# A hybrid decoder layer: one level of Strassen's algorithm for the queries and values of the last 512 tokens

## The chip, the cores and the metric

The kernel runs on one core of a Trainium2 chip. TensorE (PE) multiplies, VectorE (DVE), ScalarE (ACT) and GpSimd (POOL) do elementwise work, and SyncE (SP) issues nearly all transfers as one queue in program order. The metric is the device time of one execution in microseconds (us). A measurement of this kernel can tell about 0.2% (1.65 us) from no change.

## The reference

Each of 2048 tokens has 1024 channels, all in float32. What the change touches is the combined input projection:

```python
h = (rmsnorm(x, g_norm[l]).astype(jnp.float32) * (1.0 + scale[:, None, :]) + shift[:, None, :]).astype(x.dtype)
proj = jnp.einsum('bsd,de->bse', h, w_in[l])
gq, gk, gv, ga, gz, sq, sk, sv, sz = split_cols(proj, COL_SIZES)
...
q = rope(sq.reshape(B, S, SWA_Q_HEADS, SWA_HEAD_DIM), positions)
k = rope(sk.reshape(B, S, SWA_KV_HEADS, SWA_HEAD_DIM), positions)
o_swa = sliding_window_sink_attention(q, k, v, sinks[l])
o_swa = (o_swa.astype(jnp.float32) * jax.nn.silu(sz.astype(jnp.float32))).astype(x.dtype)
y = jnp.einsum('bse,ed->bsd', jnp.concatenate([o_gla, o_swa], axis=-1), w_out[l])
x = (x.astype(jnp.float32) + gate[:, None, :] * y.astype(jnp.float32)).astype(x.dtype)
```

`gv` holds the values (512 columns) of the gated linear attention (GLA), whose queries and keys are `gq`, `gk`, decay input `ga` and gate `gz`. `sq` holds the 512 query columns of the sliding window attention (SWA), which rope rotates; `sk`, `sv` are its keys and values and `sz` its gate.

## The kernel before

**Units and slots.** The tokens are worked through in four units of 512 (unit 0 to 3). A unit multiplies its normalized input by the columns of `w_in` in nine slots, in the order of the list `ORDER`. A slot is one group of columns: `sz0`, `sz1`, `gz0`, `gz1`, `qk0`, `qk1` (256 each, function `proj_t`, PSUM tile `pt`), `kv` (272), `sq` and `gv` (512 each, function `proj_n`, PSUM tile `pn`). After the units an output stage (`out_pair`, tiles `ya` and `ys`) multiplies by `w_out`, already by seven Strassen products in place of eight for all but the first pair of token tiles.

**Products.** Every float32 operand is split in a high and a low part of type float32r: `hh`, `hl` for the input (8 tiles of 128 channels by 512 tokens), and two parts for the weights. One product is three matmuls:

```python
def mm3(ps, lh, ll, rh, rl, first, last, bank=None):
    mmul(ps, lh, rh, first, False, bank)
    mmul(ps, lh, rl, False, False)
    mmul(ps, ll, rh, False, last)
```

So `sq` and `gv` take 4 token tiles x 8 channel tiles x 3 = 96 matmuls each in a unit, of 512 columns each. They alternate between two PSUM banks (`mm`).

**Weights.** Unit 0 splits the weights and writes the parts to DRAM (`wc`). Later units load them as tiles of 1 MB, each in two transfers, into a ring of five buffers (`w_tile`, `WB = 5`): a load waits until the last matmul that reads the tile five loads earlier.

**What follows a slot.** The queries are rotated by DVE and POOL (`rope`), the values are copied by ACT. As soon as the slots that they need are done, SWA is computed per token tile (`swa_tile`, PSUM tiles `pq`, `psc`, `ppt`, `ppo`) and GLA per pair of heads (`gla`, tiles `pk`, `pc`, `pu`, `po`, `pms`). Results go to DRAM (`mixd`). `norm` makes the next unit's `hh` and `hl`. They live in a pool of 13 buffers of each kind (`hp`, `HB = 13`): 8 for a unit, 5 for the start of the next.

**Late work.** The output stage's weights are combined at low priority inside units 1 and 2: `late_gate`, then `late_rows(k)` for k = 0 to 3, which load four blocks of `w_out` (`wor`), multiply them on DVE, form combinations on POOL, split them on ACT and DVE and store them (`woc`). The table `LATE_AT` says after which slot each piece may begin. `last_rows` loads them back (`woh`, `wol`).

**Order.** All calls are recorded (class `Order`), and a list scheduler with durations of its own fixes each engine's instruction order before the program is built. `od.lift` shifts the priority of what is recorded next. Helpers record everything, so the profile shows one line for all calls (L390) and two for PE (L441, L446); tiles tell them apart.

Of the kernel before, what the change touches and what calls it, by code (L numbers as in the profile page):

```python
# [395 lines left out]
def layer_kernel(ctx, tc, small, x, xT, w_ada, w_gate, b_gate, w_in, w_dec, w_out, g_fin, out):  # L396
# [14 lines left out]
    const = Pool("const", 1)  # L411
    hp = Pool("hp", HB)
    wp = Pool("wp", 1)
# [202 lines left out]
    def last_rows():  # L616
# [7 lines left out]
        for op in WO:  # L624
            for k in range(KT // 2):
                wo[op, k] = []
                for j in range(2):
                    name = f"wo{'hl'[j]}{op}{k}"
                    if op == WO[3] and k == KT // 2 - 3:
                        t = keep.tile([P, NB], F32R, name=name, tag="wst", bufs=4)  # L630
                    elif op == WO[3] and k >= KT // 2 - 2:
                        t = spare[:, k - KT // 2 + 2, j]
                    elif op in WO[:4]:
                        t = hp.tile([P, NB], F32R, name=name, tag=f"h{'hl'[j]}")
# [15 lines left out]
    woc = dram.tile([P, 2, len(WO), KT // 2, NB], F32R, name="woc")  # L650
    wo = {}

    def first_w():
# [197 lines left out]

    def norm(u):

# [662 lines left out]
    for i, (u, slot) in enumerate(todo):  # L1516
        if u > 0 and slot == ORDER[0]:
            hh, hl = nexth[u]
        w = ws[i]
        name, _, half = slot.partition("/")  # L1520
        if name == "kv":
            proj_n(w, SLOT_N[name], sink_kv(u))
        elif name == "sq":
            qrs[u] = {}
# [6 lines left out]
        seen.add((u, slot))  # L1531
        if half:
            if not {(u, f"{name}/{c}") for c in range(2)} <= seen:
# [6 lines left out]
        for what, g, need in (("S", 0, ("kv", "sz0", "sq")), ("S", 1, ("kv", "sz1", "sq")),  # L1540
                              ("G", 0, ("qk0", "gv", "kv")), ("G", 1, ("qk1", "gv")),
                              ("Z", 0, ("qk0", "gz0", "gv")), ("Z", 1, ("qk1", "gz1", "gv"))):
            if name in need and all((u, n) in seen for n in need):
                if what == "S":
# [10 lines left out]
        if u < NU - 1 and name == (NORM_AT if u else NORM_AT0):  # L1555
            od.lift = -LIFT
            norm(u + 1)
            od.lift = 0
        if (u, name) in LATE_AT:
            at = LATE_AT[u, name]  # L1560
            od.lift = LATE_LIFT
            late_gate() if at == "gate" else late_rows(at)
            od.lift = 0
# [58 lines left out]
```

## Time and profile before

| | |
|---|---|
| three runs | 826.36, 827.63, 827.90 us; median 827.63 us |
| the profiled execution | 827.18 us, of which the span of its instructions is 825.4 us |
| busy share of the span | PE 98%, weight loads 82%, DVE 71%, ACT 63%, POOL 43% |
| bytes moved | 200.82 MB, mean 243 GB/s |
| granted PE clock | 1.00 after the first 50 us (2.4 GHz) |

The span is what the trace covers; 1.8 us of the execution lie outside it. Unit 1 begins with slot `sz0` at 158.7 us, unit 2 at 330 us, unit 3 at 495.4 us, the output stage at 657 us. Unit 3 runs its slots at 495.4 (`sz0`), 507.0 (`kv`), 525.0 (`sz1`), 537.5 (`sq`), 559.2 (`qk0`), 574.5 (`gv`), 610.8 (`gz0`), 631.3 (`qk1`) and 643.4 (`gz1`).

### The profile page before, as it was taken

To read this page: it belongs to the slowest core of one execution; us is meant where nothing else is said; L and a number is where in the kernel's file an instruction comes from. 1 tells how busy PE (TensorE), PEld (TensorE's weight loads), DVE (VectorE), ACT (ScalarE), POOL (GpSimd) and SP (SyncE) were. 2 spreads that over 40 slices of the span, in tenths; PEclk is the share of its full clock that TensorE was granted. 3 is DMA by queue.
4 is the path that set the end of the run, shared out by engine and by line. 5 is a ranking of instruction groups with operands and counts; after the bars stand their busy time and mean duration, and the time that the engine had idled before them with its cause. 6 is when DMAs were issued, how large, how long until landed. Compare 5 with 4: busy or idle time off the path is not lost.

```text
span 825.4 us, 13307 instructions
## 1 busy us (share of the span) xinstructions
PE 809.1 (98%) x4286; PEld 674.9 (82%) x4286; DVE 587.0 (71%) x1172; ACT 519.2 (63%) x1293; POOL 353.0 (43%) x442
## 2 busy tenths in 40 slices
PE   8899999999999999999999999999999999999996
PEld 7788888898888877888887788888887888888885
DVE  6987567777578878665788836525764857898985
ACT  4769856999457786956587757615866544444432
POOL 3812325566435756446476524332562412233300
PEclk9999999999999999999999999999999999999999
DMA  9979998738285696896978937727376863454432
GB/s 356 371 262 369 383 384 300 252 125 332 90 318 204 228 374 222 264 385 230 328 240 302 325 114 267 259 82 288 122 241 246 292 244 128 154 165 150 152 107 77
DMA packets 92125, 200.82 MB, mean 243 GB/s; under 512 B 9443, under 2 KB 27414, under 8 KB 89366
## 3 DMA queue, kind: packets, MB, share of 16 engines
q1 hardware_dynamic: 91766, 199.69, 68.2%
q8 instruction: 34, 0.56, 0.3%
q14 instruction: 37, 0.30, 0.1%
q10 hardware_dynamic: 288, 0.26, 0.1%
HBM read 145.26 MB, written 54.66 MB: 242 GB/s over the span
## 4 chain that ended last, share of the span: by engine, by line
PE 80%; DVE 6%; ACT 6%; DMA 4%; issue 2%; POOL 0%; SPq 0%; DVEq 0%; ACTq 0%; POOLq 0%
PE pn L441 23%; PE pt L441 19%; PE ya L441 10%; PE ys L441 9%; PE po L441 6%; PE psc L441 3%; PE ppo L441 3%; DMA mixd<-o 2%; PE ppt L446 1%; DMA xn<-in_x 1%; DMA xt<-in_xT 1%; PE pu L441 1%; PE pc L441 1%; PE pms L441 1%; PE pq L446 1%
## 5 line engine op out<-in xcount | busy, mean ns | idle before, releaser
L441 PE MATMUL pn<-w_gv,hh 128*128 128x512 f32 x256 | 83.5, 397 | 0.0
L441 PE MATMUL pn<-w_sq,hh 128*128 128x512 f32 x256 | 81.3, 394 | 0.0
L441 PE MATMUL pt<-hh,w_gz 128*128 128x512 f32 x224 | 75.8, 399 | 0.0
L441 PE MATMUL pt<-hh,w_qk 128*128 128x512 f32 x224 | 73.9, 398 | 0.0
L441 PE MATMUL pt<-hh,w_sz 128*128 128x512 f32 x224 | 72.5, 395 | 0.1
L390 ACT ACTIVATE ge<-ge 128x512 f32<-128x512 f32 x96 | 60.6, 631 | 15.1 <-DVE ge L390 14.0
L390 ACT ACTIVATE s<-s,nm 128x129 f32<-128x129 f32 x128 | 51.2, 401 | 20.5 <-DVE nm L390 19.8
L441 PEld LDWEIGHTS pn<-w_sq,hh 128*128 128x128 f32 x256 | 47.8, 188 | 10.6 <-issue 0.3
L441 PEld LDWEIGHTS pn<-w_gv,hh 128*128 128x128 f32 x256 | 47.5, 188 | 9.6 <-ACT kvr L390 0.4
L441 PE MATMUL ys<-woht,m 128*128 128x512 f32 x168 | 53.4, 392 | 0.0
L390 POOL TENSOR_TENSOR s<-s,den 128x512 f32<-128x512 f32 x32 | 36.6, 1146 | 35.0 <-DVE den L390 33.2
L441 PE MATMUL pn<-w_gv,hl 128*128 128x512 f32 x128 | 50.8, 397 | 0.0
L441 PE MATMUL pn<-w_kv,hh 128*128 128x272 f32 x256 | 50.1, 290 | 0.0
L441 PE MATMUL pn<-w_sq,hl 128*128 128x512 f32 x128 | 50.1, 393 | 0.0
L390 POOL TENSOR_TENSOR xt<-xt,rstd 128x512 f32<-128x512 f32 x27 | 40.0, 1481 | 23.2 <-DMA xt<-in_xT 17.1
L441 PEld LDWEIGHTS pt<-hh,w_sz 128*128 128x128 f32 x224 | 41.9, 188 | 9.2 <-ACT kvr L390 0.3
L441 PEld LDWEIGHTS pt<-hh,w_gz 128*128 128x128 f32 x224 | 41.7, 188 | 8.8 <-issue 0.5
L441 PE MATMUL ya<-wohb,m 128*128 128x512 f32 x152 | 48.7, 390 | 0.0
L441 PEld LDWEIGHTS pt<-hh,w_qk 128*128 128x128 f32 x224 | 41.8, 188 | 8.0
L390 POOL TENSOR_TENSOR o<-o,zs 128x128 f32<-128x128 f32 x64 | 32.4, 525 | 29.7 <-DVE o L390 29.3
L441 PE MATMUL pt<-hl,w_qk 128*128 128x512 f32 x112 | 44.3, 396 | 0.0
L441 PE MATMUL pt<-hl,w_gz 128*128 128x512 f32 x112 | 44.1, 394 | 0.0
(288 smaller groups left out, 2314.0 us busy)
## 6 DMA issues: line engine op xcount, KB each, us to landing
w_sz<-wc SPq DMA_DIRECT2D x24, 512.0 KB, 5.7
w_sq<-wc SPq DMA_DIRECT2D x24, 512.0 KB, 6.8
w_qk<-wc SPq DMA_DIRECT2D x24, 512.0 KB, 5.2
w_gv<-wc SPq DMA_DIRECT2D x24, 512.0 KB, 8.4
w_gz<-wc SPq DMA_DIRECT2D x24, 512.0 KB, 6.2
mr<-mixd SPq DMA_DIRECT2D x32, 256.0 KB, 3.3
y<-in_x SPq DMA_DIRECT2D x32, 256.0 KB, 3.2
out<-y SPq DMA_DIRECT2D x30, 256.0 KB, 2.0
```

The lines of the kernel that those rows point to most:

```text
L390: return order.add(eng, lambda: real(*args, **kw), dur, ins, outs, lock=lock, nbytes=nbytes)
L441: return od.add("PE", lambda: T.matmul(o, l, r, start=start, stop=stop), dur, [l, r] + ([] if start else [o]), [bank if start and bank is ...
L446: return od.add("PE", lambda: T.transpose(o, i, ident), 0.109, [i, ident], [o], mode="few" if o.shape[0] <= 32 else None)
```

## The change

In unit 3 alone, the slots `sq` and `gv` become one slot, `sqgv`, right after `kv`. It sees the input as a 2x2 matrix of blocks (token tiles 0, 1 against 2, 3; even against odd channel tiles) and the weights likewise (even against odd channel tiles; `sq` against `gv`), and forms the four result blocks from seven products in place of eight:

- `late_cols(k)`, k = 0 to 3, is new late work in units 1 and 2: it loads four blocks of `sq` and `gv`, forms the four weight combinations t1 to t4 on POOL, splits them on ACT and DVE and stores both parts (`wt`). `LATE_AT` now places `late_rows(1)` to `(3)` in unit 2.
- `prepare(u)` forms the input combinations s1 to s4 on DVE from slot `sz0` on. They take the five pairs of `hp` buffers that no next unit needs: s2 and s3 are split at once, s4 and s1 wait in DRAM (`sd`) and are reloaded and split into the same buffers after product s3.
- `slot_f` loads 14 weight tiles; `proj_f` runs the seven products for two token tiles each and adds up the results.

The diff, shortened (unit 2's row of `ORDER_F` is not used, since `FAST` names unit 3 alone):

```diff
-LATE_AT = {(1, 'sz0'): 'gate', (1, 'sz1'): 0, (1, 'qk0'): 1, (1, 'gv'): 2, (1, 'qk1'): 3}
+FAST = (3,)
+ORDER_F = {2: [...], 3: ['sz0','kv','sqgv','sz1','qk0','gz0','qk1','gz1']}
+AGAIN_LIFT = 800
+PREP_LIFT = 400
+PREP_AT = 'sz0'
+SEVEN = (("a11", "b11"), ("a12", "b21"), ("s2", "t2"), ("s3", "t3"), ("a22", "t4"), ("s1", "t1"), ("s4", "b22"))
+LATE_AT = {(1,'sz0'):'gate',(1,'sz1'):0,(1,'sq'):4,(1,'gv'):5,(1,'qk1'):6,(2,'sz0'):7,(2,'sz1'):1,(2,'gv'):2,(2,'gz0'):3}
...
+    def late_cols(k):
+        b = {}
+        for r, c in ((0, 0), (0, 1), (1, 1), (1, 0)):
...
+            SY.dma_start(b[r, c], src[:, 2 * k + r])
+        def part(op, to, x, y):
+            G.tensor_tensor(to, x, y, ALU.subtract)
+            parts = [stp.tile([P, NB], F32R, name=f"wt{j}{op}{k}", tag="st") for j in "xy"]
+            A.copy(parts[0], to)
+            V.tensor_tensor(parts[1], to, f(parts[0]), ALU.subtract)
+            for j in range(2):
+                SY.dma_start(f(wt[:, int(op[1]) - 1, k // 2, k % 2, j]), f(parts[j]))
...
+    def prepare(u):
...
+        def split(t, names, i):
+            h_, l_ = to = homes[2 * i:2 * i + 2]
+            A.copy(h_, t)
+            V.tensor_tensor(l_, t, f(h_), ALU.subtract)
...
+        def first():
+            for i in range(KT // 2):
+                x1, x2 = [stp.tile([P, NB], F32, name=f"S{i}{c}{u}", tag="xs", bufs=2) for c in range(2)]
+                for k, x_ in ((2 * i + 1, x2), (2 * i, x1)):
+                    V.tensor_tensor(x_, f(hh[k]), f(hl[k]), ALU.add)
+                V.tensor_tensor(x2[:, hi], x1[:, hi], x2[:, hi], ALU.add)
+                V.tensor_tensor(x1[:, hi], x1[:, lo], x1[:, hi], ALU.subtract)
+                V.tensor_tensor(x1[:, lo], x2[:, hi], x1[:, lo], ALU.subtract)
+                split(x1, ("s2", "s3"), i)
+                V.tensor_tensor(x2[:, lo], x2[:, lo], x1[:, lo], ALU.subtract)
+                SY.dma_start(sd[u][:, i], x2)
+        def second():
+            for i in range(KT // 2):
+                x2 = stp.tile([P, NB], F32, name=f"S{i}2{u}", tag="xs", bufs=2)
+                SY.dma_start(x2, sd[u][:, i])
+                split(x2, ("s4", "s1"), i)
...
+        def done(a, p, ps):
+            if a == "a11":
+                U[p] = combos["U"][p]
+                A.copy(U[p], ps)
...
+            elif a == "a12":
+                V.tensor_tensor(o, ps, o if split_c11 else U[p], ALU.add)
+                turned(p)
+            elif a == "s2":
+                V.tensor_tensor(U[p], ps, U[p], ALU.add)
+            elif a == "s3":
+                V.tensor_tensor(value(2 + p), ps, U[p], ALU.add)
+            elif a == "a22":
+                V.tensor_tensor(query(2 + p), ps, flat(2 + p), ALU.add)
+                turned(2 + p)
+            elif a == "s1":
+                V.tensor_tensor(value(p), ps, U[p], ALU.add)
+                V.tensor_tensor(flat(2 + p), ps, flat(2 + p), ALU.add)
+            else:
+                V.tensor_tensor(flat(p), ps, flat(p), ALU.add)
...
+        for n, (a, _) in enumerate(SEVEN):
...
+            for p in range(2):
+                ps = mm.tile([P, NB], F32, name=f"pf{n}{p}", tag="mm")
+                for k in range(KT // 2):
+                    mm3(ps, *left(a, k, p), w(0, n, k), w(1, n, k), k == 0, k == KT // 2 - 1)
+                    if p == 1 and k % 2:
+                        ahead(1)
+                od.lift = -LIFT
+                done(a, p, ps)
+                od.lift = 0
```

On PE, the place is unit 3's product with the queries' weights. Before, token tile after token tile runs through the eight channel tiles (`hh_0`, `hl_0` and so on) against one of four weight tiles (`w_sq`); the PSUM tile is `pn`.

```order
L441 MATMUL pn_1383<-w_sq_0_1365,hh_0_1196 128x512 x2
L441 MATMUL pn_1383<-w_sq_0_1365,hl_0_1197 128x512
L441 MATMUL pn_1383<-w_sq_0_1365,hh_1_1199 128x512 x2
L441 MATMUL pn_1383<-w_sq_0_1365,hl_1_1200 128x512
L441 MATMUL pn_1383<-w_sq_1_1366,hh_2_1202 128x512 x2
L441 MATMUL pn_1383<-w_sq_1_1366,hl_2_1203 128x512
```

In the change, the rows where product a12 (`pf_1450`) ends and product s2 (`pf_1455`) begins. `Shh` and `Shl` are the parts of an input combination, `w_t` is a weight combination, `po` belongs to GLA of the unit before.

```order
L454 MATMUL pf_1450<-w_b_1_1434,hh_7_1378 128x512 x2
L454 MATMUL pf_1450<-w_b_1_1434,hl_7_1379 128x512
L454 MATMUL pf_1455<-w_t_0_1435,Shh_1384 128x512 x2
L454 MATMUL po_1355<-sT,v 128x128 x4
L454 MATMUL pf_1455<-w_t_0_1435,Shl_1385 128x512
L454 MATMUL pf_1455<-w_t_0_1435,Shh_1386 128x512 x2
L454 MATMUL pf_1455<-w_t_0_1435,Shl_1387 128x512
L454 MATMUL pf_1455<-w_t_1_1445,Shh_1388 128x512 x2
L454 MATMUL pf_1455<-w_t_1_1445,Shl_1389 128x512
L454 MATMUL pf_1455<-w_t_1_1445,Shh_1390 128x512 x2
L454 MATMUL pf_1455<-w_t_1_1445,Shl_1391 128x512
```

The left operand of the third product now comes from DVE and ACT of the same unit, and GLA of unit 2 runs between the products.

On DVE, the rows of the change that end in the last part that s2 needs (`Shl_1391`), with the drains of a12 (`qr<-pf`) among them; `rope` and `qr` rotate a query, `S` are the combinations.

```order
L397 TENSOR_TENSOR S_1401<-hh_7_1378,hl_7_1379 128x512
L397 TENSOR_TENSOR rope_1439<-kvr,sin 128x2x32
L397 TENSOR_TENSOR S_1401<-S_1400,S_1401 128x256
L397 TENSOR_TENSOR rope_1439<-kvr,sin 128x2x32
L397 TENSOR_TENSOR S_1400<-S_1400 128x256
L397 TENSOR_TENSOR qr<-pf_1447,Shh_1392 128x512
L397 TENSOR_TENSOR S_1400<-S_1401,S_1400 128x256
L397 TENSOR_TENSOR rope_1449<-qr,sin 128x8x32
L397 TENSOR_TENSOR S_1401<-S_1401,S_1400 128x256
L397 TENSOR_TENSOR rope_1449<-qr,sin 128x8x32
L397 TENSOR_TENSOR Shl_1391<-S_1400,Shh_1390 128x512
```

Before, DVE has at the `sq` slot only the rotation of each token tile (`qr<-pn`, `rope<-pn`).

On SP, the loads around the slot. Before, four query tiles and then the next slots' tiles:

```order
L390 DMA w_sq_0_1365<-wc 128x1024 x2
L390 DMA w_sq_1_1366<-wc 128x1024 x2
L390 DMA w_sq_2_1367<-wc 128x1024 x2
L390 DMA mixd<-qk_1277 128x4x128
L390 DMA w_sq_3_1376<-wc 128x1024 x2
L390 DMA mixd<-qk_1280 128x4x128
L390 DMA w_qk_0_1380<-wc 128x1024 x2
```

In the change, with the spills (`sd<-S`) and reloads (`S<-sd`) of s4 and s1 between the tiles:

```order
L397 DMA w_b_0_1407<-wc 128x1024 x2
L397 DMA sd_104<-S_1395 128x512
L397 DMA sd_104<-S_1397 128x512
L397 DMA w_b_1_1432<-wc 128x1024 x2
L397 DMA w_b_0_1433<-wc 128x1024 x2
L397 DMA w_b_1_1434<-wc 128x1024 x2
L397 DMA sd_104<-S_1399 128x512
L397 DMA w_t_0_1435<-wt 128x1024 x2
L397 DMA w_t_1_1445<-wt 128x1024 x2
L397 DMA w_t_0_1446<-wt 128x1024 x2
L397 DMA sd_104<-S_1401 128x512
L397 DMA S_1465<-sd_104 128x512
```

Three spills and a reload now stand ahead of weight tiles that PE needs, where before only two stores of GLA did.

## Rows read from the trace of the kernel before

**Rows 1.** The page: busy time of each engine with its share of the span, and the granted PE clock in 40 equal slices of the span (tenths of full speed).

```profile
PE 809.1 (98%) x4286; PEld 674.9 (82%) x4286; DVE 587.0 (71%) x1172; ACT 519.2 (63%) x1293; POOL 353.0 (43%) x442
PEclk9999999999999999999999999999999999999999
```

**Rows 2.** Waits of PE over the whole span: for whom, us in total, times, longest.

```profile
PE po L441 <- ACT hh L390: 2.2, 2, 2.1
PE pw L441 <- POOL ones_r L390: 2.1, 1, 2.1
PE pk L446 <- DVE pl L390: 1.4, 1, 1.4
PE ppo L441 <- ACT ph L390: 1.2, 1, 1.2
PE pk L446 <- DVE qk L390: 0.5, 1, 0.5
PE po L441 <- DVE o L390: 0.4, 1, 0.4
PE pms L441 <- ACT osq L390: 0.4, 1, 0.4
PE psc L441 <- DVE s L390: 0.3, 1, 0.3
```

**Rows 3.** The chain of work that ended last, in order of time: start us, us, what. Pieces of unit 3: GLA inside slot `kv`, the whole slot `sq`, a piece of SWA.

```profile
512.61 1.09 PE pc L441 x16
516.75 0.89 PE po L441 x8
521.64 1.98 PE po L441 x24
529.37 0.46 PE pms L441 x2
537.62 21.76 PE pn L441 x96
562.38 0.95 PE psc L441 x8
```

**Rows 4.** Busy time by stretch (us from the span's start): length, then busy us of PE, PEld, DVE, ACT, POOL with instruction counts, granted clock, DMA share, GB/s. In order: `kv`, part of `sz1` and `gv` of unit 2, unit 3's `sz0`, `kv`, `sq`, then the start and the body of the output stage.

```profile
345.80:357.90 12.10, 12.10 (x98) 12.06 (x98) 10.87 (x28) 9.74 (x26) 4.28 (x7) 1.00 1.04 368
363.00:375.00 12.00, 12.00 (x83) 10.23 (x82) 4.98 (x15) 4.55 (x8) 4.94 (x8) 1.00 1.00 389
414.00:444.40 30.40, 30.40 (x157) 25.38 (x156) 26.03 (x46) 25.07 (x71) 23.61 (x25) 1.00 0.69 233
495.40:507.00 11.60, 11.60 (x52) 9.55 (x51) 7.57 (x14) 8.33 (x15) 4.02 (x3) 1.00 1.02 342
507.00:525.00 18.00, 18.00 (x165) 17.14 (x164) 10.50 (x31) 10.58 (x24) 8.05 (x14) 1.00 0.42 143
537.50:559.20 21.70, 21.70 (x97) 17.93 (x96) 4.49 (x10) 2.99 (x5) 6.86 (x8) 1.00 0.30 99
657.10:700.00 42.90, 42.90 (x207) 35.49 (x206) 26.59 (x52) 20.24 (x44) 9.00 (x8) 1.00 0.60 208
700.00:815.00 115.00, 115.00 (x503) 94.15 (x502) 98.17 (x188) 49.08 (x121) 27.44 (x20) 1.00 0.40 135
```

**Rows 5.** The same view of the stretch before unit 2 in which DVE is busiest.

```profile
267.00:279.00 12.00, 11.71 (x64) 9.80 (x63) 11.39 (x23) 9.15 (x26) 7.07 (x8) 1.00 0.44 146
```

**Rows 6.** Groups of instructions by form: engine, operation, out<-in, shapes, count | busy us, mean ns of one | idle before and releasers. The first reads one operand from PSUM, the others of DVE read both from SBUF.

```profile
L390 DVE TENSOR_TENSOR y<-ya,y 128x512 f32<-128x512 f32 x50 | 33.5, 686 | 10.9 <-PE ya L441 10.2
L390 DVE TENSOR_TENSOR hl<-xt,hh 128x512 fp32r<-128x512 f32 x27 | 22.5, 833 | 11.9 <-ACT xt L390 9.6 <-PE pt L441 2.2
L390 DVE TENSOR_TENSOR hl<-xt,hh 128x256 fp32r<-128x256 f32 x2 | 0.8, 424 | 1.4 <-ACT xt L390 1.4
L390 DVE TENSOR_TENSOR wor<-wor,gate 128x512 f32<-128x512 f32 x16 | 14.5, 923 | 0.1
L390 DVE TENSOR_TENSOR woyt<-wor,woxt 128x512 fp32r<-128x512 f32 x16 | 13.0, 814 | 0.2
L390 DVE TENSOR_TENSOR qk<-qk,en 128x512 f32<-128x512 f32 x8 | 8.9, 1115 | 1.9 <-ACT en L390 1.9
L390 ACT CAST woxt<-wor 128x512 fp32r<-128x512 f32 x16 | 9.9, 616 | 1.4 <-POOL wor L390 1.3
L390 ACT COPY v<-pn 128x512 f32<-128x512 f32 x16 | 9.3, 579 | 2.5 <-PE pn L441 2.5
L390 POOL TENSOR_TENSOR wor<-wor,wor 128x512 f32<-128x512 f32 x16 | 23.4, 1467 | 11.7 <-ACT ge L390 4.2 <-DVE woyt L390 4.2 <-DVE woyb L390 3.3
```

**Rows 7.** Transfers: the loads of `w_sq` in unit 3 (ns of the issue min/median/max, first and last issue) and their time from issue to landing; the same for one of the stores of `late_rows`; then, for the whole run, issues by form with KB each and median us to landing.

```profile
L390 SPq DMA_DIRECT2D w_sq<-wc x8: 319/406/436, 521.7 to 532.1; - x8
DMA to landing us min/median/max: 6.5/7.8/9.0
L390 SPq DMA_DIRECT2D woc<-woyt x16: 319/320/1194, 288.4 to 461.5; - x16
w_sq<-wc SPq DMA_DIRECT2D x24, 512.0 KB, 6.8
w_gv<-wc SPq DMA_DIRECT2D x24, 512.0 KB, 8.4
woc<-woxt SPq DMA_DIRECT2D x16, 256.0 KB, 3.2
```

More of the change, by code (lines that the diff above doesn't have):

```diff
@@ L57 @@
 ORDER = ['sz0', 'kv', 'sz1', 'sq', 'qk0', 'gv', 'gz0', 'qk1', 'gz1']
[L58 removed]
+FAST = (3,)
+ORDER_F = {2: ['sz0','kv','sz1','sqgv','qk0','gz0','qk1','gz1'], 3: ['sz0','kv','sqgv','sz1','qk0','gz0','qk1','gz1']}
+STATS_AT = 0
+AGAIN_LIFT = 800
[3 more added lines that the diff above has]
+LATE_AT = {(1,'sz0'):'gate',(1,'sz1'):0,(1,'sq'):4,(1,'gv'):5,(1,'qk1'):6,(2,'sz0'):7,(2,'sz1'):1,(2,'gv'):2,(2,'gz0'):3}
 WO = ("b11", "b21", "t1", "b22", "t2", "t3", "t4")
@@ L411, in layer_kernel, with h_tile @@
     const = Pool("const", 1)
-    hp = Pool("hp", HB)
+    hp = Pool("hp", 1)
+    h_next = {"hh": 0, "hl": 0}
+    def h_tile(name, kind):
+        h_next[kind] += 1
+        return hp.tile([P, NB], F32R, name=name, tag=f"{kind}{(h_next[kind] - 1) % HB}")
     wp = Pool("wp", 1)
@@ new lines, in slot_f, with load @@
+    def slot_f(u):
+        tiles = {}
+        kept = {"b11": ("sq", 0), "b21": ("sq", 1), "b22": ("gv", 1)}
+        def load(n, j):
+            op = SEVEN[n][1]
+            t = w_tile(f"w_{op}{u}_{j}").rearrange("p (k i m) -> p k i m", i=2, k=2)
+            tiles[n, j] = t
+            od.lift = -LIFT
+            for k in range(2):
+                if op in kept:
+                    name, at = kept[op]
+                    src = kept_of(name)[:, 2 * j + k, at]
+                else:
+                    src = wt[:, int(op[1]) - 1, j, k]
+                SY.dma_start(f(t[:, k]), f(src))
+        stream.extend([lambda n=n, j=j: load(n, j) for n in range(7) for j in range(2)])
+        return lambda i, n, k: tiles[n, k // 2][:, k % 2, i]
@@ new lines, in prepare @@
+    def prepare(u):
+        homes = [hp.tile([P, NB], F32 if i == HB - KT - 1 else F32R, name=f"S{kind}{i}{u}",
+                         tag=f"{kind}{(h_next[kind] + i) % HB}")
+                 for i in range(HB - KT) for kind in ("hh", "hl")]
+        lo, hi = slice(0, NB // 2), slice(NB // 2, NB)
+        combos = {"U": homes[-2:]}
+        def split(t, names, i):
+            h_, l_ = to = homes[2 * i:2 * i + 2]
+            A.copy(h_, t)
+            V.tensor_tensor(l_, t, f(h_), ALU.subtract)
+            for op, part in zip(names, (lo, hi)):
+                combos[op, i] = [x[:, part] for x in to]
+        def first():
[14 more added lines that the diff above has]
+                split(x2, ("s4", "s1"), i)
+        od.lift = -PREP_LIFT
+        first()
+        od.lift = 0
+        return combos, second
@@ new lines, in rope_in_place @@
+    def rope_in_place(q, t):
+        r2 = tmp.tile([P, 8, 64], F32, name="rope2", tag="rope2", bufs=1)
+        c = cos[:, t].unsqueeze(1).broadcast_to([P, 16, 32])
+        s = sin[:, t].unsqueeze(1).broadcast_to([P, 8, 32])
+        lo, hi = slice(0, 32), slice(32, 64)
+        for a, b in ((lo, hi), (hi, lo)):
+            V.tensor_tensor(r2[:, :, a], q[:, :, b], s, ALU.mult)
+        halves_ = q.rearrange("p h (a b) -> p (h a) b", a=2)
+        V.tensor_tensor(halves_, halves_, c, ALU.mult)
+        for a, op in ((lo, ALU.subtract), (hi, ALU.add)):
+            G.tensor_tensor(q[:, :, a], q[:, :, a], r2[:, :, a], op)
@@ L875, in norm @@
         A.copy(r, pr)
+        scale_of[u] = r
+    def norm(u):
+        if u not in scale_of:
+            stats(u)
+        r = scale_of[u]
         nh, nl = [], []
@@ L1531, in layer_kernel @@
         seen.add((u, slot))
+        seen |= {(u, n) for n in ("sq", "gv") if name == "sqgv"}
         if half:
@@ L1542, in layer_kernel @@
                               ("Z", 0, ("qk0", "gz0", "gv")), ("Z", 1, ("qk1", "gz1", "gv"))):
-            if name in need and all((u, n) in seen for n in need):
+            if (name in need or name == "sqgv") and all((u, n) in seen for n in need):
                 if what == "S":
@@ L1558, in layer_kernel @@
             od.lift = 0
-        if (u, name) in LATE_AT:
-            at = LATE_AT[u, name]
+        if (u, slot) in LATE_AT:
+            at = LATE_AT[u, slot]
             od.lift = LATE_LIFT
-            late_gate() if at == "gate" else late_rows(at)
+            for n in at if isinstance(at, tuple) else (at,):
+                late_gate() if n == "gate" else late_rows(n) if n < 4 else late_cols(n - 4)
             od.lift = 0
```

77 lines of the change are left out of this document (67 added, 10 removed).

## The prediction

> **What bounds the kernel now.** I read the page first. PE is busy 98% of the span at a granted clock of 1.00, that is the 2.4 GHz level [rows 1]. Matmuls overlap, so a busy PE could hide stalls. The chain of waits settles that. It holds slot `sq` of unit 3 as one piece of 96 matmuls in 21.76 us [rows 3], 226.7 ns each, and the stretch view shows no PE idle time there (21.70 of 21.70 us, rows 4). The list of PE's waits comes next. All waits after the first 30 us are short: 1.4, 1.2, 0.5, 0.4, 0.4 and 0.3 us, 4.2 us together [rows 2]. So the time is PE's instruction stream, and a matmul less there is its pitch less, as long as what feeds PE keeps up.
>
> In slot `sq` of unit 3 the other engines rest: DVE works 4.5 us of 21.7, ACT 3.0, and DMA runs at 99 GB/s [rows 4]. Much of the new work lands there.
>
> **What the change takes away.** Unit 3's `sq` and `gv` are 192 matmuls of 512 columns. Seven products of two token tiles, four channel tiles and three matmuls are 168. 24 x 226.7 ns = **5.44 us** come off PE's stream. Nothing is added on PE. The order of instructions is the same up to slot `qk1` of unit 1, near 300 us, so the first third should not move.
>
> **What it adds to feed PE in unit 3.** On DVE: 8 sums of `hh` and `hl`, 16 combinations of half width, 8 low parts, 14 drains of PSUM. I price a drain as `y<-ya,y` (686 ns), a half as the 128x256 `hl` (424 ns), and an instruction that reads twice from SBUF as `hl` (833 ns) [rows 6]: 8 x 0.833 + 16 x 0.424 + 8 x 0.833 + 14 x 0.686 = 29.7 us. ACT gets 8 casts and 2 drains and loses 4 copies of values: 8 x 0.616 - 2 x 0.579 = 3.8 us. The rotation keeps its three DVE and two POOL instructions per tile.
>
> Of this, only the first part has a deadline. PE needs the four parts of s2 after `sz0`, `kv`, a11 and a12. In the trace before, `sz0` and `kv` take 29.6 us, of which DVE works 7.57 + 10.50 = 18.1 us [rows 4]; a11 and a12 add 2 x 24 x 0.2267 = 10.9 us. That leaves 29.6 - 18.1 + 10.9 = 22.4 us of DVE. By the order, it has to hold 8 sums, 16 halves, 4 low parts, one drain, a rotation and some late work (two `wor<-wor,gate` and two low parts, 2 x 0.923 + 2 x 0.814 us). That is 6.7 + 6.8 + 3.3 + 0.7 + 1.5 + 3.5 = 22.5 us: DVE would be full. Uncontended, at 686 ns for each instruction that reads twice from SBUF, it is 20.1 us. A DVE at 95% costs PE 0.3 us in 12 us [rows 5]. The sums need only `hh` and `hl`, which PE itself needs, so the work can begin early. I take **1.0 us** of PE waiting at s2. Below, nothing; above, 12 such instructions at the dearest row (`qk<-qk,en`, 1115 ns) are 12 x 0.28 = 3.4 us more, so 4 us.
>
> A rule speaks against this part. Rows first: with one operand in PSUM an instruction of 512 columns takes 686 ns, with both in SBUF 814 to 1115 ns [rows 6]. The Trainium skill (SBUF — State Buffer, section Who interferes with whom) says that a DVE instruction with two SBUF inputs contends with a GpSimd instruction that reads SBUF, as a lock: the later one waits until the earlier is done. The spread of these rows agrees. By that rule a sum that meets a POOL instruction waits up to that one's length, 1467 ns in the row of `wor`, and three such meetings on the way to s2 would be the 4 us above.
>
> **Transfers.** The 8 tiles of `sq` and `gv` become 14. From the start of the first product to the start of `sz1`, the order has 12 of the 14 tiles, `sz1`'s two, and 1.6 MB of spills and reloads: 14 x 1.05 + 1.6 = 16.3 MB. PE's time for it is 168 x 0.2267 = 38.1 us, and the pieces of GLA and SWA that are interleaved, 1.09 + 0.89 + 1.98 + 0.92 + 0.95 us by the rows plus transposes of about 0.9, so 44.8 us [rows 3]. That asks for 364 GB/s. Saturated stretches moved 342, 368 and 389 GB/s [rows 4]: at 389 the loads are hidden, at 368 just so, at 342 they take 47.7 us, 2.9 us too long. The loads start with little lead, since the ring of five still holds `kv`'s tiles, and a tile takes 6.5 to 9.0 us from issue to landing [rows 7]. I take **1.5 us**, between 0 and 4, and half a microsecond less than the sum of this and the wait at s2, since they overlap: 2.0 us for both. The Trainium skill (DMA: Bandwidth & Descriptors, section Specifications) names about 358 GB/s as a core's share of HBM. By that figure the slot's loads would need 45.5 us, 0.7 us too long; 389 GB/s in a stretch here is above it.
>
> **Late work.** `late_cols` is 4 POOL, 4 ACT and 4 DVE instructions and 12 transfers per piece, 4 x 0.814 = 3.3 us of DVE; a piece of `late_rows` is 4 x 0.923 + 7 x 0.814 = 9.4 us. Before, the stores of `late_rows` ran from 288 to 461 us [rows 7]. Now 13 us of DVE work goes in front of three of its four pieces, and by the order the last store comes in unit 3's slot `qk1`. Cover: `gv` of unit 2 has DVE at 26.0 of 30.4 us [rows 4], so there is room, but not much. All waits above but one of 0.3 us fall behind 300 us, where the order first differs, so 4 us can be gained or replaced. I take nothing, with -2.5 and +2 as bounds: the waits of unit 1 (1.4, 0.5, 0.4 us) vanish, or as much is added in unit 2. If the cover fails, a late piece costs nothing by itself, but it delays product drains on DVE.
>
> The GLA of the last pair of heads now begins behind the first output products. That moves some 10 us of DVE work there. The output stage's first 42.9 us have DVE at 26.6 us [rows 4], so it is hidden; later, at 98 of 115 us, it would not all be.
>
> **Sum.** 827.18 (profiled) - 5.44 + 2.0 + 0 = 823.7 us. The profiled run is 0.45 us under the median of the runs, so **824.0 us** with rounding.
>
> **Rivals.**
> 1. *The gain comes whole, and old waits go too.* For it: the rest of DVE and DMA in slot `sq`, lighter late work in unit 1. Against it: 364 GB/s. -5.44 - 2 gives 820.2 us.
> 2. *s2 comes late.* The lock of the two ports makes the way to s2 dear: 4 us there, and 1 us of transfers behind it. 827.63 - 5.44 + 5 = 827.2 us: no change.
> 3. *The transfer queue.* SP issues in order, and spills and reloads stand ahead of weight tiles at three places (the first two spills, the last spill with the first reload, the last two reloads). At each, the tile behind is issued only once DVE is done. The lead that is left is one product and a quarter, 24 x 0.2267 + 1.4 = 6.8 us; a landing takes up to 9.0 us [rows 7]. Three times 2.2 us and 1.0 us at s2 are 7.6 us: 829.8 us, slower. It decides from 7.1 us of waits on, that is when each place loses over 2 us.
> 4. *Given back in the output stage.* If GLA's last part slips into its body, DVE, at 85% there, delays the sums `y`, and PE waits 4 us for banks: 826.5 us. For it: the order. Against it: the first 43 us have room.
>
> **Chances.** My forecast (822 to 826 us) 0.56; rival 1 0.14; rival 2 0.14; rival 3 0.11; rival 4 0.05. Slower by over 0.2% (above 829.3 us) needs rival 3 with its waits as priced: 0.11, and 0.01 for the tail of rival 2. Faster by over 0.2% (below 826.0 us): the forecast, rival 1, and 0.02 from the edge of rival 2: 0.72. The rest, 0.16, is no measurable change. 0.2% is what a measurement of this kernel can tell. The range that holds 8 in 10 goes from 820.5 us (half of rival 1) to 828.5 us (rivals 2 and 4 with the bound of the transfers); the forecast's own is 822 to 826 us.
>
> **What would show it.** Right: PE's `pf` matmuls at 227 ns, 168 of them, no difference before 290 us, PE waits in unit 3 under 3 us in total, DMA at 350 GB/s or more through the slot. Wrong on s2: a PE wait for `Shl` or `Shh` of over 3 us, with DVE busy throughout. Wrong on transfers: PE waits for `w_t` or `w_b`, and SP waits for DVE `S`. Wrong on late work: new PE waits between 400 and 495 us. Wrong on the output stage: PE waits for `y` after 660 us. The prediction fails as a whole if these waits pass 5 us together.

## The result, and the profile after

The change took **822.08 us** (median of four runs, 821.77 to 824.01) against 827.36 us (826.36 to 827.90, four runs of the kernel before beside it). The ratio is 0.9942, with a 95% interval from 0.9924 to 0.9961. It is faster by more than the 0.2% that a measurement can tell. I had forecast 824.0 us, from 820.5 to 828.5, faster with 0.72. The profiled execution took 822.16 us, its span is 820.4 us, 5.0 us under that of the kernel before.

The page's row of busy time after the change, which answers to [rows 1]: busy us, share of the span, instructions.

```profile
PE 803.6 (98%) x4262; PEld 669.0 (82%) x4262; DVE 626.8 (76%) x1234; ACT 528.0 (64%) x1315; POOL 377.7 (46%) x458
```

PE has 24 instructions less and is as full as before. DVE, ACT and POOL have 40, 9 and 25 us more, and none became the bound. The list of PE's waits over the whole span (for whom, us in total, times, longest), to be held against [rows 2]:

```profile
PE po L454 <- ACT hh L397: 2.3, 2, 2.1
PE pw L454 <- POOL ones_r L397: 2.1, 1, 2.1
PE pf L454 <- DMA w_b<-wc: 1.7, 1, 1.7
PE pk L459 <- DVE qk L397: 1.2, 1, 1.2
PE po L454 <- DVE Q L397: 0.4, 1, 0.4
PE pt L454 <- ACT kvr L397: 0.3, 1, 0.3
PE psc L454 <- DVE s L397: 0.3, 1, 0.3
...
```

The account, first up to 300 us. There both kernels have the same order of instructions, and PE is at the same matmul at 300.82 us before and at 300.90 us now: nothing is gained. Two differences cancel each other. The change's profile has 1.4 us of small waits in unit 0 (rows for `pt`, `pz`, `ppt`, `gaT` and `pn`, at 64 to 150 us). The profile before has a stretch of lower clock that the change's has not (columns as in [rows 4]; first before, then the change):

```profile
25.00:30.00 5.00, 5.00 (x18) 3.95 (x17) 5.00 (x8) 3.41 (x8) 5.00 (x5) 0.72 1.04 417
25.00:30.00 5.00, 5.00 (x24) 4.14 (x23) 5.00 (x8) 3.34 (x8) 5.00 (x5) 1.00 1.03 410
```

PE does 18 matmuls before and 24 now in the same 5 us. Both are scatter between executions.

Behind 300 us, 24 matmuls give -5.4 us. In units 1 and 2, PE waited 1.4 + 1.2 + 0.5 + 0.4 = 3.5 us before; now 1.2 + 0.4 = 1.6 us, so -1.9. Unit 3 had one wait of 0.4 us and has one of 1.7 us for `w_b`, a weight tile of the first product: +1.3. The sum is -6.0 us, and the profiles show -5.1. The 0.9 us between them stand in no row of waits; where they went is not shown.

Stretches of the change (us from the start; then as in [rows 4]): the whole slot `sqgv`, and 60 us of the output stage.

```profile
518.50:566.20 47.70, 45.99 (x239) 37.48 (x237) 37.29 (x73) 20.32 (x43) 19.48 (x22) 1.00 1.00 369
700.00:760.00 60.00, 60.00 (x263) 49.12 (x263) 54.24 (x107) 25.80 (x66) 19.07 (x14) 1.00 0.57 189
```

The slot runs with DMA busy throughout at 369 GB/s and loses 1.7 us of PE in 47.7. These 60 us of the output stage have DVE at 54.24 us and PE without a gap.

The one new wait, in the chain of waits of that stretch (start us, us, what):

```profile
515.29 0.44 DVE S L397
...
515.75 0.32 SPq L397
...
516.16 6.03 DMA w_b<-wc
...
522.24 1.89 PE pf L454 x7
```

DVE ends a combination, SP can issue the store of it, behind that stands the second weight tile, and its first half lands 6.03 us later.

### The profile page after: what moved, and what is told of

Same layout as the page of the kernel before. It is cut to its first block, busy times and chain, and to the rows that moved or that the text cites. A ratio compares the mean times of both kernels' runs of the same rounds, so it can differ in the third digit from the quotient of the medians.

```text
span 820.4 us, 13492 instructions
## 1 busy us (share of the span) xinstructions
PE 803.6 (98%) x4262; PEld 669.0 (82%) x4262; DVE 626.8 (76%) x1234; ACT 528.0 (64%) x1315; POOL 377.7 (46%) x458
## 2 busy tenths in 40 slices
DMA packets 101917, 221.79 MB, mean 270 GB/s; under 512 B 10531, under 2 KB 28502, under 8 KB 99158
## 4 chain that ended last, share of the span: by engine, by line
PE 76%; DMA 7%; DVE 4%; ACT 4%; issue 2%; POOL 1%; SPq 1%; DVEq 0%; POOLq 0%; ACTq 0%
PE pt L454 23%; PE pn L454 15%; PE ya L454 10%; PE ys L454 9%; PE pf L454 5%; PE ppo L454 3%; PE psc L454 3%; PE po L454 2%; PE ppt L459 2%; DMA xt<-in_xT 1%; DMA xn<-in_x 1%; PE pc L454 1%; PE pms L454 1%; DMA wr_gv<-in_w_in 1%; PE pu L454 1%
## 5 line engine op out<-in xcount | busy, mean ns | idle before, releaser
L454 PE MATMUL pn<-w_gv,hh 128*128 128x512 f32 x192 | 62.0, 397 | 0.2 <-ACT kvr L397 0.2
L454 PE MATMUL pn<-w_sq,hh 128*128 128x512 f32 x192 | 61.7, 395 | 0.0
L454 PE MATMUL pt<-hl,w_sz 128*128 128x512 f32 x112 | 44.4, 396 | 0.0
L397 POOL TENSOR_TENSOR qr<-qr,rope 128x256 f32<-128x256 f32 x32 | 26.4, 846 | 35.4 <-DVE rope L397 25.7
L454 PEld LDWEIGHTS pn<-w_sq,hh 128*128 128x128 f32 x192 | 35.8, 188 | 8.1 <-issue 0.3
L454 PEld LDWEIGHTS psc<-kst,qs 128*128 128x128 f32 x256 | 37.7, 188 | 5.5 <-DVE s L397 1.0
```

The source lines that it names most:

```text
L397: return order.add(eng, lambda: real(*args, **kw), dur, ins, outs, lock=lock, nbytes=nbytes)
L454: return od.add("PE", lambda: T.matmul(o, l, r, start=start, stop=stop), dur, [l, r] + ([] if start else [o]), [bank if start and bank is ...
```

## The experiments

The list scheduler makes a new order for each kernel, so most edits move more than they name. The traces show how much. The repetition of the change has the change's order on every engine. The kernel with four matmuls moved differs from it on PE alone. The slot alone keeps the order of the kernel before up to 494 us. The others differ on all engines, among them the one without the stores from 505 us, with tiles loaded twice from 533 us, with half of the tiles from 537 us and with the sums twice from 495 us. What those runs cost or gave is the price of the edit with its new order.

### Late work and slot apart

Theory after the result: the slot gives its 24 matmuls less the wait for `w_b`, and the moved late work takes about 2 us of waits away. The rival: it is all the slot's.

**The late work alone**, without the Strassen slot:

```diff
-FAST = (3,)
+FAST = ()
```

> The change with all its late work (late_cols and the moved late_rows; the stored combinations are read by nobody), but with sq and gv as before in unit 3. It prices the late work alone, and against the change the slot alone. Theory: 4286 matmuls, the waits between 300 and 495 us as in the change (1.6 us), so 822.1 + 5.44 - 1.7 + 0.4 = 826.2 us, that is 1.2 us under the kernel before. Rival: the late work costs or gives nothing by itself, 827.4 us; or it costs DVE time, 828 us and more.

Measured: 825.07 us against 828.06, ratio 0.9965 (0.9950 to 0.9979). Its waits behind 300 us, the 0.4 for `o` in unit 3:

```profile
PE pk L459 <- DVE qk L397: 1.2, 1, 1.2
PE pt L454 <- ACT kvr L397: 0.5, 1, 0.5
PE po L454 <- DVE o L397: 0.4, 1, 0.4
PE po L454 <- DVE Q L397: 0.4, 1, 0.4
```

So 2.1 us in units 1 and 2 where there were 3.5. The profiled execution gained 0.7 us of span (824.7 us), the medians say 2.9 us; that execution (826.39 us) is 1.3 us over its median. That late work by itself makes the kernel faster is shown; how much is not.

**The pieces of `late_rows` moved, and nothing else** (in the kernel before):

```diff
-LATE_AT = {(1, 'sz0'): 'gate', (1, 'sz1'): 0, (1, 'qk0'): 1, (1, 'gv'): 2, (1, 'qk1'): 3}
+LATE_AT = {(1, 'sz0'): 'gate', (1, 'sz1'): 0, (2, 'sz1'): 1, (2, 'gv'): 2, (2, 'gz0'): 3}
```

> The kernel before with late_rows(1) to (3) moved to unit 2 as in the change, no new late work and no Strassen slot. The change has 1.6 us of PE waits between 300 and 495 us where the kernel before has 3.5 us. Theory: the moved pieces alone take them away, since DVE is less loaded in unit 1: PE waits of 317 to 360 us fall from 2.3 to under 1 us, the time to some 825.5 us. Rival: the waits hang on the order of GLA and the normalization and not on late work; 827.4 us as before.

Measured: 828.12 us against 828.06, ratio 0.9989 (0.9971 to 1.0007), no difference that can be told. The waits at 317 and 338 us went (1.4 and 0.4 us), but PE now waits 1.4 and 0.7 us at 357 us and 0.9 us at 426 us. My theory for the waits fell here: moving the pieces moves the waits, and how many are left depends on the whole order.

**The slot alone**, and the change again beside it:

```diff
-LATE_AT = {(1,'sz0'):'gate',(1,'sz1'):0,(1,'sq'):4,(1,'gv'):5,(1,'qk1'):6,(2,'sz0'):7,(2,'sz1'):1,(2,'gv'):2,(2,'gz0'):3}
+LATE_AT = {(1, 'sz0'): 'gate', (1, 'sz1'): 0, (1, 'qk0'): 1, (1, 'gv'): 2, (1, 'qk1'): 3}
...
-                if op in kept:
-                    name, at = kept[op]
+                if True:
+                    name, at = kept.get(op, ("gv", 0))
```

> The Strassen slot alone: late_rows where the kernel before has them, no late_cols; the slot's t tiles are loaded from other weights of the same size, so that the output is of other numbers. With the run of the late work alone (0.9965) it splits the change's 0.994. Theory A (the sum of my prediction, with the measured wait): 24 matmuls less (-5.44 us), +1.7 us for w_b, and the waits of units 1 and 2 as before: -3.7 us, 0.9955; then late work and slot add up to more than the change shows, or the late work's part is 1.3 us. Theory B (the late work's -2.9 us is whole, and the slot gives -1.9 us because work is pushed into the output stage): 0.9977.

> The change itself, beside the next two on the same chip and against the same runs of the kernel before, so that slot, late work and change are compared with each other. Expected 0.994 of the kernel before, as before.

Measured: the slot alone 0.9941 (0.9918 to 0.9963), the change 0.9943 (0.9922 to 0.9964). Waits of the slot alone behind 300 us:

```profile
PE pk L459 <- DVE pl L397: 1.4, 1, 1.4
PE pk L459 <- DVE qk L397: 1.2, 1, 1.2
PE ppo L454 <- ACT ph L397: 0.9, 2, 0.6
```

The old waits of units 1 and 2 are there (3.5 us), and there is none for `w_b`. The order up to 494 us is that of the kernel before, yet single waits differ: 0.6, 1.4, 1.2 and 0.3 us here against 1.4, 0.4, 0.5 and 1.2. So one row moves by up to 0.9 us from execution to execution, and the sum came out the same in these two.

Theory B is outside the interval. Theory A's number (0.9955) is inside, but its term of 1.7 us for `w_b` did not come; without it 24 matmuls less are 0.9934, inside as well. So the slot alone gives what its matmuls say, within the interval. It is worth as much as the whole change, 4.9 us, and late work and slot don't add up (0.9965 x 0.9941 = 0.9906). Of that difference of 3 us the wait for `w_b`, 1.2 to 1.7 us in the two profiles of the change, appears only when both are there; the next section shows how. The rest is within what the three intervals leave, and stays open.

### What makes PE wait for `w_b`

Theory: the ring of five is still held by `kv`'s four tiles, so the second tile can't come much earlier. Rivals: the store that stands ahead of it in SP's queue, and the bytes of the slot.

**Without the stores** of s4 and s1:

```diff
-                SY.dma_start(sd[u][:, i], x2)
...
-                SY.dma_start(x2, sd[u][:, i])
+                SY.dma_start(f(x2), f(wc[:, i * NB:(i + 1) * NB]))
```

> The change without the four stores of the combinations s4 and s1 to DRAM; the reloads read other data of the same size, so the last products are of other numbers. It tests what stands ahead of the weight tiles in SP's queue. In the change, the second tile of b11 is issued at 516.2 us, right behind a store that waited 9.7 us for DVE, and the fourth combination waits 2.9 us for a store to land. Theory: the ring's buffer comes free only near 515.2 us, so without the store the tile comes at most 1 us earlier, and the PE wait falls from 1.7 us to between 0.7 and 1.7 us; s2 has slack, so nothing else changes: 821.1 to 822.1 us. Rival (head of the queue is all): the tile is issued at 505.6 us and the wait is gone, 820.4 us.

Measured: 822.79 us, 0.9937 (0.9917 to 0.9957). PE's one wait in the first products, and the matmuls of the slot from the seventh on, which read the second tile (start us, us, what; in brackets the idle time before and what ended it):

```profile
PE pf L454 <- ACT Shh L397: 0.9, 1, 0.9
```

```profile
520.27 0.63 PE L454 MATMUL pf<-w_b,hh 128*128 128x512 f32 x2
...
522.76 0.74 PE L454 MATMUL pf<-w_b,hh 128*128 128x512 f32 x2 [0.95 <-ACT Shh L397]
```

The second tile is issued at 515.1 us, and PE goes on to it at 520.27 us without a gap: the wait for it is gone. The 0.9 us is another wait, for ACT's copy of a finished bank, which stands behind a cast of a combination. It takes back part of the gain, and the time is the change's within the intervals.

So theory and rival were each half right. The buffer sets the earliest issue: SP waits for PE up to 515.1 us, not 505.6. But PE would not have waited for a tile issued then. In the change SP waits 9.7 us for DVE's combination instead and issues the store at 515.75 us and the tile 0.4 us behind it; its first half then took 6.03 us to land, and 5.0 to 5.6 us in four other runs with the store in this place. In the slot alone the store was issued at 513.84 us and had landed at 516.01, before the tile was issued at 517.47 us, and the tile landed within 4.0 us. There DVE has no late work any more, while in the change five instructions of it (`woyb`, `wor`, `woyt`, 3.4 us) stand among the combinations, and DVE waits 1.2 us for the first store to land. So the wait comes only with slot and late work together: the combination is later, its store stands right ahead of the tile, and the tile loses about 1 us before its issue and 1 to 2 us on the way. That it is the late work that makes the combination late is read from these two traces; no run tests it by itself.

**`sz1` between `kv` and the products:**

```diff
-3: ['sz0','kv','sqgv','sz1','qk0','gz0','qk1','gz1']
+3: ['sz0','kv','sz1','sqgv','qk0','gz0','qk1','gz1']
```

> The change with the slots of unit 3 in the order sz0, kv, sz1, sqgv. My theory of the one new PE wait of the change (1.7 us for w_b at 522 us): the weight tiles of the first products come late because the buffers of the ring are still held by kv's tiles, and not because too many bytes are moved in the slot. With sz1 between kv and the products, four of their tiles are loaded while sz1 computes (11.5 us), and the wait goes: no PE wait for w_b over 0.3 us, some 820.4 us against 822.1. The rival, bandwidth: the slot asks for as many bytes as before, so a wait of 1 to 2 us comes later in the slot, for w_t or w_b: 822 us.

Measured: 827.87 us, 0.9996 (0.9983 to 1.0009). The wait for `w_b` is gone, as the theory had it; PE waits 0.6 us for `w_t` in all. But the whole gain of the change is gone too. The profiled execution (829.75 us) is the second slowest of twelve, from 825.44 to 829.89 us; its mean granted clock is 0.991, where the seven fastest have 0.995 or 0.996. PE's waits in the output stage, the chain there, and the stretches behind two of those waits (columns as above):

```profile
PE ya L454 <- DVE y L397: 3.5, 2, 2.8
PE pms L454 <- ACT osq L397: 0.7, 1, 0.7
```

```profile
662.62 0.33 SPq L397
...
663.00 3.39 DMA mixd<-qk
...
666.46 4.35 DMA y<-in_x
...
670.83 0.70 DVE y L397
...
671.58 1.45 PE ya L454 x5
```

```profile
656.30:659.20 2.90, 2.90 (x8) 2.30 (x7) 0.05 (x1) 0.72 (x2) 0.00 (x0) 0.50 0.01 4
673.20:676.20 3.00, 3.00 (x8) 2.31 (x7) 2.59 (x3) 0.70 (x2) 2.92 (x3) 0.50 0.00 0
```

GLA of the last pair reaches further into the output stage; its store `mixd<-qk` is late, SP issues the load of `y` only when that store has landed, DVE can't drain a bank of `ya` without it, and PE stops for 2.8 us. After each of these stops PE ran at half clock for some 3 us (0.50, the level of 1.2 GHz). This is my fourth rival, in a kernel that differs from the change by the place of one slot. What the faster executions lost, which have a higher clock, is not shown.

**Four matmuls moved.** In the change, PE stops at the ninth matmul of the slot, which needs the late tile, while four on the tile that is there stand behind it:

```diff
-            for p in range(2):
-                ps = mm.tile([P, NB], F32, name=f"pf{n}{p}", tag="mm")
-                for k in range(KT // 2):
+            pss = [mm.tile([P, NB], F32, name=f"pf{n}{p}", tag="mm") for p in range(2)] if n == 0 else None
+            for p, ks in ((0, (0, 1)), (1, (0, 1)), (0, (2, 3)), (1, (2, 3))) if n == 0 else ((0, range(4)), (1, range(4))):
+                ps = pss[p] if n == 0 else mm.tile([P, NB], F32, name=f"pf{n}{p}", tag="mm")
+                for k in ks:
```

> The change with four matmuls of the first product moved: those of the second token tile on the weight tile that is there (hl_0, hh_2 twice, hl_2 against w_b_0) now stand ahead of the first four on the tile that is late (w_b_1). No other instruction on any engine changes its place. In the change, PE stops at the ninth matmul of the slot, while four that could run stand behind it. Theory: the transfer lands at the same time, so the wait for w_b shrinks by 4 x 0.227 = 0.9 us, from 1.2 to 1.7 us to between 0.3 and 0.8 us, and the time by 0.9 us: 0.993 of the kernel before. Rival: the wait is set by what comes later in the slot, and 0.9 us returns at the next tile: 0.994.

Measured: 0.9931 (0.9914 to 0.9948), 823.04 us against 828.68, and

```profile
PE pf L454 <- DMA w_b<-wc: 0.3, 1, 0.3
```

The wait shrank as expected: what is left is for the second half of the same tile, and no later one came in the slot. The time saved is not shown. The profiled span is 819.5 us, 0.9 under the change's, but in it a wait of 0.9 us for `pt` came in unit 2, where the order is the change's, and most of the small waits of unit 0 went. The medians can't tell so little.

**Half of the t tiles not loaded:**

```diff
-                SY.dma_start(f(t[:, k]), f(src))
+                if op in kept or k == 0:
+                    SY.dma_start(f(t[:, k]), f(src))
...
-        return lambda i, n, k: tiles[n, k // 2][:, k % 2, i]
+        return lambda i, n, k: tiles[n, k // 2][:, k % 2 if SEVEN[n][1] in kept else 0, i]
```

> The change without half of the loads of the t tiles (each tile loads its first half, and the matmuls of the second half read the first one): 4.2 MB less in the slot, with 168 matmuls as before; the result is of other numbers. Theory: the wait for w_b comes ahead of the t tiles and hangs on when the buffers of kv come free, so it stays at 1.2 to 1.7 us, and nothing else waits for transfers now: 822 us, 0.994. Rival: the slot's bytes are the bound and the wait is their sign; it goes, 820.5 us.

Measured: 0.9953 (0.9937 to 0.9969), 824.06 us. The wait for `w_b` is 0.7 us, smaller than I had expected it to stay; new ones of 0.8 us for `ya` and 0.4 us for a later product stand against that. The tile's first half took 5.0 us to land here, against 6.0, with the same order up to that place, and so the shorter wait is scatter. With 4.2 MB less nothing is gained in the whole, so no cost of these bytes is to be seen; since the order changes from 537 us on, a small one could be hidden.

### How near the edge it is

**More bytes:** t2 and t3 loaded twice.

```diff
-                SY.dma_start(f(t[:, k]), f(src))
+                for again in range(2 if op in ("t2", "t3") else 1):
+                    SY.dma_start(f(t[:, k]), f(src))
```

> The change with each tile of t2 and t3 loaded twice into its buffer (2.1 MB more in the slot, 5.7 us at the 369 GB/s that the slot moves in the change). It tells how near the slot is to the bound of its transfers. Theory: it is at the bound (DMA share 1.00 for 47.7 us), so PE waits for weight tiles rise from 1.7 us to between 5 and 7 us: 826 us. Rival: the lead of five tiles still hides most of it: under 2 us more, 823 us.

Measured in one run: 835.17 us, 12 us over the change beside it (823.21), where theory had 4 and the rival 1. The largest of PE's waits:

```profile
PE pf L454 <- DMA w_t<-wt: 3.0, 3, 1.1
PE pq L459 <- DVE kst L397: 2.8, 1, 2.8
PE psc L454 <- DVE qs L397: 1.7, 1, 1.7
```

PE waits for tiles, and then 2.8 and 1.7 us for operands of SWA that are late in turn. Theory had the direction, and its size rested on a wrong count. The edit loads four tiles of 1 MB again, that is 4.2 MB and not 2.1: the page has 225.99 MB against 221.79. At 369 GB/s they take 11.4 us, near to what the run lost. One execution can't tell the two numbers apart.

**More DVE work ahead of s2:**

```diff
-                    V.tensor_tensor(x_, f(hh[k]), f(hl[k]), ALU.add)
+                    for again in range(2):
+                        V.tensor_tensor(x_, f(hh[k]), f(hl[k]), ALU.add)
```

> The change with each of the eight sums of hh and hl computed twice on DVE, 8 x 0.69 = 5.5 us more DVE work ahead of product s2. My prediction gave 1.0 us of PE waiting at s2, and the change shows none. In its trace the last part that s2 needs is done at 534.2 us and read at 536.2 us, and DVE idles for 2.9 us at 526.4 us (behind a store of the combinations), so about 5 us are free. Theory (slack of about 5 us): PE waits for Shh or Shl stay under 1 us, 822 to 823 us. Rival (DVE is at its limit, as I predicted): the 5.5 us show in full at s2, 827 us or more.

Measured: 825.32 us, 0.9966 (0.9953 to 0.9979). By the ratios that is 2 us over the change (0.9943), with intervals that still meet. No wait at s2. The time went to other places:

```profile
PE pf L454 <- ACT kvr L397: 1.5, 1, 1.5
PE pk L459 <- DVE qk L397: 1.3, 1, 1.3
PE pf L454 <- DVE v L397: 0.7, 1, 0.7
PE pf L454 <- DVE Shl L397: 0.5, 1, 0.5
```

s2 had the slack that my theory gave it; the price showed where DVE's other customers are late (GLA's `qk`, the drains). Time and place of the cost I had both wrong.

**`kv` ahead of `sz0`:**

```diff
-3: ['sz0','kv','sqgv','sz1','qk0','gz0','qk1','gz1']
+3: ['kv','sz0','sqgv','sz1','qk0','gz0','qk1','gz1']
...
-PREP_AT = 'sz0'
+PREP_AT = 'kv'
...
-        if u > 0 and slot == ORDER[0]:
+        if u > 0 and slot == (ORDER_F[u] if u in FAST else ORDER)[0]:
```

> The change with kv ahead of sz0 in unit 3 (the preparation recorded at kv). The last product's order against the output stage stays as in the change. If the wait for w_b comes from kv's four tiles that hold the ring, it goes, since kv's buffers are loaded again while sz0 computes; and the output stage has no new waits, as it had with sz1 ahead. Theory: 1.7 us under the change, 820.4 us, 0.992. Rival: the preparation comes later or DVE is fuller by then, and PE waits for Shh or Shl instead: 822 us or more.

Measured: 831.32 us, 1.004 (1.0023 to 1.0057), slower than the kernel before. The end of the chain in front of PE's longest wait, and three stretches:

```profile
512.02 0.61 DVE dd L397
...
513.20 0.61 ACT en L397
513.81 0.28 ACT kvr L397
...
514.13 2.07 PE pt L454 x4
```

```profile
500.00:505.00 5.00, 4.35 (x33) 3.91 (x32) 5.00 (x14) 4.86 (x12) 1.00 (x3) 1.00 0.59 212
505.00:510.00 5.00, 4.09 (x33) 3.86 (x31) 4.97 (x13) 1.42 (x4) 1.74 (x2) 1.00 0.47 127
514.70:519.40 4.70, 4.70 (x12) 3.63 (x11) 4.30 (x10) 1.18 (x4) 3.22 (x5) 0.50 1.00 363
```

The wait for `w_b` is gone here too. But now DVE is full (5.00 and 4.97 of 5 us) while `kv`'s results want to be rotated. ACT waits for DVE's `dd` with GLA's exponentials (`en`), its copy of `kvr` stands behind them, and PE stops 5.0 us for the bank that this copy frees. Then it runs at half clock for 4.7 us. The rival was right that DVE is fuller by then, and by more than it said; but PE waits only 0.3 us for `Shh`, and the price is paid at `kv`'s bank.

**Late work earlier:**

```diff
-LATE_AT = {(1,'sz0'):'gate',(1,'sz1'):0,(1,'sq'):4,(1,'gv'):5,(1,'qk1'):6,(2,'sz0'):7,(2,'sz1'):1,(2,'gv'):2,(2,'gz0'):3}
+LATE_AT = {(1,'sz0'):'gate',(1,'sz1'):0,(1,'sq'):1,(1,'qk0'):4,(1,'gv'):5,(1,'gz0'):6,(1,'qk1'):7,(2,'sz0'):2,(2,'sz1'):3}
```

> The change with another table for the late work: gate, rows 0 and 1 and all four column pieces in unit 1, rows 2 and 3 from the start of unit 2, so that less of it is left when unit 3's slot begins. The slot alone (late_rows as in the kernel before) had no wait for w_b and 5.44 + 0.2 us less. Theory: late work that reaches into unit 3 delays w_b and DVE there; with it earlier the wait shrinks under 1 us, 820.5 to 821.5 us. Rival: it now loads DVE in units 1 and 2, where the waits of the kernel before return (up to 2 us): 822 to 823 us.

Measured: 836.33 us, 1.0096 (1.0081 to 1.0112), by the ratios some 13 us over the change. PE stands for 9.5 us in front of GLA's transposes. The chain of that stretch:

```profile
509.06 7.74 DMA woc<-woyb
...
516.90 0.63 ACT woxt L397
...
517.55 1.65 DVE woyt L397
...
520.62 5.89 DMA sd<-S
...
529.22 0.61 DVE qk L397
...
529.88 1.12 PE pk L459 x4
```

A store of output weights takes 7.74 us to land, a piece of late work waits for its buffer and holds ACT and DVE, the store of s4 and s1 that follows takes 5.89 us, behind two halves of a weight tile that were issued up to 1 us ahead of it, the next sum on DVE waits for its buffer, and GLA's `qk` is behind that sum. Neither theory nor rival had this. It is my third rival's queue, at a price that I had not thought of: the wait for one store's landing, handed on through two engines in order.

## Why the prediction was right, point by point

- **24 matmuls, -5.44 us:** right. PE has 24 instructions less, and the slot alone, with the old waits, gave 4.9 us (0.9941; 5.44 us are 0.9934).
- **s2, 1.0 us:** there was none, the step was mis-sized. The work was as I priced it (16.8 us for sums, halves and four low parts). In the change, on DVE from 490 to 536 us (busy us, mean ns of one):

```profile
L397 DVE TENSOR_TENSOR S<-hh,hl 128x512 f32<-128x512 f32 x8 | 6.6, 822 | 4.2 <-DMA sd<-S 4.1
L397 DVE TENSOR_TENSOR S<-S,S 128x256 f32<-128x256 f32 x12 | 6.1, 510 | 0.1
L397 DVE TENSOR_TENSOR Shl<-S,Shh 128x512 fp32r<-128x512 f32 x4 | 2.9, 718 | 0.0
L397 DVE TENSOR_TENSOR S<-S 128x256 f32<-128x256 f32 x4 | 1.7, 415 | 0.0
```

  That is 17.3 us. What I had too small was the room. I counted 22.5 us of work in 22.4 us. From the first sum at 492.0 us to PE's reading of the last part at 536.2 us it was 44.2 us where I had 40.5, 1.7 of them the wait for `w_b`. The rest of DVE's work took 20.3 us in it where I had 23.8. So in the trace DVE even stood 4.1 us for stores of its own combinations, and the last part was done at 534.2 us, 2.0 us before PE read it. My bound of 4 us came from the dearest row; three meetings under the lock would have given as much. Two instructions did meet POOL, a sum at 492.0 us (1796 ns against a median of 686) and a half at 519.8 us (1462 against 416). That is the rule of the Trainium skill (SBUF — State Buffer, section Who interferes with whom), and the trace agrees: a POOL instruction of 1634 and 1274 ns ran at the same time. The 2.2 us fell into the slack.
- **Transfers, 1.5 us:** 1.7 us in one profile and 1.2 us in the other, so the size was right. The reason was only half right. The little lead behind `kv`'s tiles is there, but what made PE wait was the store ahead of the tile, the first of the three places that I had given to rival 3. My other reason, the rate, was not what cost: the slot had asked for 364 GB/s and got 369, over a longer time (47.7 us against 44.8) and so with 17.6 MB where I had counted 16.3. The Trainium skill (DMA: Bandwidth & Descriptors, section Specifications) names about 358 GB/s as a core's share; 369 over 47.7 us is above it, so the measurement decides. But there was not much to spare, as the tiles loaded twice show.
- **Late work, 0 us:** mis-sized. The change's waits in units 1 and 2 fell by 1.9 us, within the bound of 2.5; half of my first rival came true. Why this order has fewer is not shown: the pieces of `late_rows` moved alone took none of the time away. The runs show that such waits move about with the order, so I could not have read their sign from the trace.
- **Output stage, nothing:** right. DVE is at 54 of 60 us there, and PE did not wait.
- **The sum:** -5.44 + 1.3 - 1.9 = -6.0 us of matmuls and waits, against my -3.4; the profiles show -5.0, the medians -5.3. The forecast was 1.9 us too high, mostly by the late work, and both misses are on the same side. The sum's own terms give 824.2 rather than 824.0 us. That 822.08 us still lies in the forecast's 822 to 826 us, by 0.1 us, is luck: single executions of the change went from 821.77 to 825.47 us. That it lies in the whole range is not.
- **The rivals** that I gave 0.30 together (s2 late, queue, output stage) did not come in the change at the size that I gave them; rival 3's queue came at one of its three places, at 1.2 to 1.7 us in place of 2.2. Two of them came in kernels with the same 168 products and another order: the output stage with `sz1` first, the queue with the late work earlier. DVE too full by the preparation came as well, with `kv` first, though ahead of `sz0` and not at s2.

## What to carry to other kernels

Where PE is full, the count of its instructions is a good first sum. But the margin is in the order: kernels with the same products took from 822 to 836 us. So look at what stands behind a waiting instruction on each engine and on the queue of transfers, and follow one late store through to PE before the order of slots or of late work is changed. The cheapest step here was to put four matmuls whose operands had arrived ahead of four whose operands had not: the wait fell from 1.2 to 1.7 us to 0.3 us, though a gain of 0.9 us is too small for these medians to show.

## What the runs showed of the hardware that I had not expected

In the trace before, the granted clock was 1.00 from 50 to 800 us, and I priced each wait at its own length. After PE had stood for 5.0 us (`kv` first) the granted clock was 0.50 for 4.7 us: 12 matmuls in a stretch that would have held 20 at 226.7 ns, some 2 us more. After 2.8 us in the output stage (`sz1` first) it was 0.50 for 3.0 us, and after two stops of 0.7 and 0.8 us close together for 2.9 us. After the 1.7 us in the change the granted clock of the whole slot is 1.00, and PE did not slow down. Even the same stop has two outcomes: near 23 us PE stands 2.1 us in front of `po` in the profiles before and after, and behind it the clock of 25 to 30 us is 0.72 in the one and 1.00 in the other. So several stops cost more than their length, and a wait has no fixed price. The Trainium skill (TensorE: Matmul & The Clock Gate, Part 1) says that an idle array is put to 1.2 GHz and that activity releases it; the two levels in these rows agree.
